# Loading pairs of row slabs as two 64-partition halves in a column-mean kernel

## Chip, cores and metric

The kernel runs on 1 core of one Trainium2 chip. The metric is device time in microseconds (us) of one launch. Three runs of the kernel before took 628.69, 629.22 and 629.66 us; the median is 629.22 us.

## The reference

```python
def setup_inputs():
    return {"x": np.random.randn(8192, 8192).astype(np.float32)}

def reference(x):
    return np.mean(x, axis=0)
```

The input is 8192 rows of 8192 floats, 268.4 MB, and each byte is read once. The output is one row of 8192 column means.

## The kernel before

The 8192 rows are seen as 64 slabs of 128 rows. Slabs are taken in pairs: 31 pairs (`n_pairs`, k = 0 to 30), and the last two slabs are handled by a separate tail.

A pair lives in one tile `pair` of 128 partitions by 16,384 floats (64 KB in each partition). Partition p holds two neighbouring rows of x, 2p and 2p + 1 of the pair's 256 rows, one after the other, so what one partition takes is 64 KB in one piece in memory. The pool `pair_pool` has 3 buffers, and the tail's tile is taken from the same pool.

The loop over k (lines 92 to 103) does three things for each pair. First, SyncE issues the pair's load (line 98). Most pairs are one load of 8 MB over all 128 partitions. Pair 0 is cut at column 2048 (`FIRST`), and the last three pairs (`BY_ROW`, k = 28 to 30) are cut at column 8192, into the first and the second row of each partition. Second, VectorE adds the first half of the previous pair to the first half of this pair. Third, except for the last pair, VectorE adds the second half of this pair onto its first half. Both adds work on 128 x 8192 floats (helper `add`, line 87). After the loop the running sum is in the first half of the last pair.

The load of pair k goes into the buffer that pair k - 3 had. That buffer is free when the first add of pair k - 2 has read it. The instructions stand in program order on each engine (`manual_schedule`), and all loads stand on SyncE's queue, q1.

The tail (lines 106 to 118) loads the second last slab in column pieces, among them one of 120 rows and one of 8 rows for columns 7680 to 8192 (`ROWS`, `SPLIT`, line 113), and the last slab in seven pieces of falling width (`PIECES`, line 116). TensorE multiplies the running sum and the tail's slabs by ones (line 65) to sum over partitions in PSUM; ScalarE and VectorE scale by 1/8192 (lines 80 and 82), and three small stores write the output.

Of the kernel before, what the change touches and what calls it, by code (L numbers as in the profile page):

```python
# [1 line left out]

# [4 lines left out]

F32 = mybir.dt.float32
ADD = mybir.AluOpType.add
GROUPS = 4  # L10

WIDE = (2048, 2048, 2048, 1024)
NARROW = (256, 256, 256, 256)
PIECES = (4096, 2048, 1024, 512, 256, 160, 96)
FIRST = 2048
BY_ROW = 3

ROWS = 120  # L20
SPLIT = 7680


@with_exitstack
def kernel(
    ctx: ExitStack,
    tc: tile.TileContext,
    x: bass.AP,
    out: bass.AP,
):  # L30
    nc = tc.nc
    P = nc.NUM_PARTITIONS
    R, C = x.shape
    n_slabs = R // P
    n_pairs = n_slabs // 2 - 1
    N0 = sum(WIDE)
    assert n_slabs % 2 == 0 and n_pairs >= 4 and N0 + sum(NARROW) == sum(PIECES) == C
    inv_r = 1.0 / float(R)

    const_pool = ctx.enter_context(tc.tile_pool(name="const", bufs=1))  # L40
    pair_pool = ctx.enter_context(tc.tile_pool(name="pair", bufs=3))
    psum_pool = ctx.enter_context(
        tc.tile_pool(name="acc", bufs=1, space=bass.MemoryType.PSUM)
    )
    res_pool = ctx.enter_context(tc.tile_pool(name="res", bufs=1))


    ctx.enter_context(tc.manual_schedule())

    ones = const_pool.tile([P, 32], F32)  # L50
    nc.gpsimd.memset(ones, 1.0)  # L51

    wide, lo = [], 0
    for n, w in enumerate(WIDE):
        bank = psum_pool.tile([P, w // GROUPS], F32, name=f"wide{n}", tag=f"wide{n}")
        wide.append((lo, w, bank))
        lo += w
    narrow = []
    for n, w in enumerate(NARROW):
        bank = psum_pool.tile([P, 512], F32, name=f"narrow{n}", tag=f"narrow{n}")  # L60
        narrow.append((lo, w, 32 * n, bank))
        lo += w

    def mm(dst, src, **flags):
        nc.tensor.matmul(out=dst, lhsT=ones, rhs=src, skip_group_check=True, **flags)  # L65

    def fold_wide(n, src, **flags):
        lo, w, bank = wide[n]
        q = w // GROUPS
        for g in range(GROUPS):  # L70
            a = lo + g * q
            mm(bank[32 * g : 32 * g + 32, :], src[:, a : a + q], **flags)

    def fold_narrow(n, src, lo, hi, **flags):
        at, _, g, bank = narrow[n]
        mm(bank[g : g + 32, lo - at : hi - at], src[:, lo:hi], **flags)

    def scaled(dst, src, eng):
        if eng == "act":
            nc.scalar.mul(out=dst, in_=src, mul=inv_r)  # L80
        else:
            nc.vector.tensor_scalar(  # L82
                out=dst, in0=src, scalar1=inv_r, scalar2=None, op0=mybir.AluOpType.mult
            )

    def add(dst, a, b):
        nc.vector.tensor_tensor(out=dst, in0=a, in1=b, op=ADD)  # L87

    before = None
    for k in range(n_pairs):
        pair = pair_pool.tile([P, 2 * C], F32, tag="pair")
        src = x[2 * P * k : 2 * P * (k + 1), :].rearrange("(p j) c -> p (j c)", j=2)
        cut = FIRST if k == 0 else C if k >= n_pairs - BY_ROW else 2 * C
        for lo, hi in ((0, cut), (cut, 2 * C)):
            if lo < hi:
                nc.sync.dma_start(out=pair[:, lo:hi], in_=src[:, lo:hi])  # L98
        if before is not None:
            add(pair[:, 0:C], pair[:, 0:C], before[:, 0:C])  # L100
        if k < n_pairs - 1:
            add(pair[:, 0:C], pair[:, 0:C], pair[:, C : 2 * C])
        before = pair


    tail = pair_pool.tile([P, 2 * C], F32, tag="pair")
    r = (n_slabs - 2) * P
    slab, last = tail[:, 0:C], tail[:, C : 2 * C]
    parts = [(lo, lo + w) for lo, w, _ in wide[:3]] + [(wide[3][0], C)]
    for lo, hi in ((0, C // 2), (C // 2, SPLIT)):  # L110
        nc.sync.dma_start(out=slab[:, lo:hi], in_=x[r : r + P, lo:hi])
    for a, b in ((0, ROWS), (ROWS, P)):
        nc.sync.dma_start(out=slab[a:b, SPLIT:C], in_=x[r + a : r + b, SPLIT:C])
    lo = 0
    for w in PIECES:
        nc.sync.dma_start(out=last[:, lo : lo + w], in_=x[r + P : R, lo : lo + w])
        lo += w


    for lo, hi in parts:  # L120
        add(before[:, lo:hi], before[:, lo:hi], before[:, C + lo : C + hi])
    lo, hi = parts[3]
    add(before[:, lo:hi], before[:, lo:hi], slab[:, lo:hi])

    rw = res_pool.tile([P, 3 * 512], F32, name="rw")
    r3 = res_pool.tile([P, WIDE[3] // GROUPS], F32, name="r3")
    row = res_pool.tile([1, C - N0], F32, name="row")

    def close(n):
        fold_wide(n, last, start=False, stop=True)  # L130
        scaled(rw[:, n * 512 : (n + 1) * 512] if n < 3 else r3, wide[n][2], "act")

    for n in range(3):
        fold_wide(n, before, start=True, stop=False)
        fold_wide(n, slab, start=False, stop=False)
    fold_wide(3, before, start=True, stop=False)
    for n, (lo, w, _, _) in enumerate(narrow):
        fold_narrow(n, before, lo, lo + w, start=True, stop=False)
    for n in range(4):
        close(n)  # L140
    W3 = 3 * GROUPS * 512
    nc.gpsimd.dma_start(  # L142
        out=out[0:W3].rearrange("(n g w) -> g n w", g=GROUPS, w=512),
        in_=rw.rearrange("(g r) (n w) -> g r n w", r=32, w=512)[:, 0],
    )
    nc.sync.dma_start(
        out=out[W3:N0].rearrange("(g w) -> g w", g=GROUPS),
        in_=r3.rearrange("(g r) w -> g r w", r=32)[:, 0],
    )
    for n, (lo, w, g, bank) in enumerate(narrow):  # L150
        if n < 3:
            fold_narrow(n, last, lo, lo + w, start=False, stop=True)
        else:
            cut = C - PIECES[-1]
            fold_narrow(n, last, lo, cut, start=False, stop=True)
            fold_narrow(n, last, cut, C, start=False, stop=True)
        scaled(row[0:1, lo - N0 : lo - N0 + w], bank[g : g + 1, 0:w], "act" if n % 2 else "dve")
    nc.sync.dma_start(out=out[N0:C], in_=row)


# [1 line left out]
_INS = ['x']  # L162
_OUTS = [((8192,), 'float32')]


# [23 lines left out]
```

## Time and profile before

| what | value |
|---|---|
| timed runs (median; lowest to highest) | 629.22 us; 628.69 to 629.66 us |
| span of the profiled execution, first to last instruction | 627.3 us |
| time around the span, taken as median less span | 1.9 us |
| DMA engines | near fully busy throughout; 428 GB/s over the span |
| VectorE busy | 533.5 us, 85% of the span |
| TensorE busy | 13.0 us, 2% |
| pair loads (line 98) | 35, of which 27 are of 8 MB |
| granted TensorE clock | 0.999 |

The profile states a span for the profiled execution and no separate device time, so its own time is taken as 627.3 us plus the 1.9 us that the median of the timed runs stands above it.

In the profile's page, section 2 cuts the span into 40 equal slices and gives the bytes moved per second in each; section 3 gives the DMA queues; section 4 follows the chain of work that ended last; section 5 lists groups of instructions with what ended the idle time before them; section 6 lists the DMA issues. The trace also holds a record of every DMA packet with its start, length and bytes; a packet here is one run of bytes that one of the 16 DMA engines moves.

### The profile page before, as it was taken

How to read it: one execution, taken by the hardware profiler on the slowest of the kernel's cores; microseconds unless marked ns; L12 is line 12 of the kernel's file. 1: busy time of each engine (PE TensorE's matmuls, PEld its weight loads, DVE VectorE, ACT ScalarE, POOL GpSimd, SP SyncE). 2: the span in 40 equal slices, each digit the busy share in tenths (PEclk: the TensorE clock that was granted, in tenths of full speed). 3: DMA queues.
4: the chain of work that ended last, by engine and by line, in shares of the span. 5: the costliest groups of instructions: out<-in, count | busy, mean ns of one | idle time of the engine just before them, and what ended most of it. 6: DMA issues, size and time to landing. Idle time of an engine off the chain costs nothing.

```text
span 627.3 us, 451 instructions
## 1 busy us (share of the span) xinstructions
PE 13.0 (2%) x106; PEld 3.8 (1%) x106; DVE 533.5 (85%) x67; ACT 4.2 (1%) x7; POOL 1.0 (0%) x6
## 2 busy tenths in 40 slices
PE   0000000000000000000000000000000000000016
PEld 0000000000000000000000000000000000000001
DVE  0538988889888899888898888988889888899994
ACT  0000000000000000000000000000000000000001
POOL 0000000000000000000000000000000000000000
PEclk9999999999999999999999999999999999999999
DMA  9999999999999999999999999999999999999997
GB/s 414 396 460 401 468 401 468 401 451 418 443 426 430 439 426 443 418 451 410 460 405 464 401 468 401 468 402 468 401 468 401 468 401 468 401 433 435 435 421 287
DMA packets 6548, 268.50 MB, mean 428 GB/s; under 512 B 900, under 2 KB 1160, under 8 KB 1553
## 3 DMA queue, kind: packets, MB, share of 16 engines
q1 hardware_dynamic: 6497, 268.45, 99.2%
q0 software_dynamic: 48, 0.02, 0.0%
q8 instruction: 1, 0.02, 0.0%
q14 instruction: 2, 0.02, 0.0%
HBM read 268.44 MB, written 0.03 MB: 428 GB/s over the span
## 4 chain that ended last, share of the span: by engine, by line
DMA 77%; DVE 22%; PE 0%; issue 0%; SPq 0%; ACT 0%; DVEq 0%
DMA pair<-in_x_dram 72%; DVE pair L87 22%; DMA tail<-in_x_dram 5%; PE narrow L65 0%; SPq L98 0%; PE wide L65 0%; ACT row L80 0%; DVEq L87 0%
## 5 line engine op out<-in xcount | busy, mean ns | idle before, releaser
L87 DVE TENSOR_TENSOR pair<-pair 128x8192 f32<-128x8192 f32 (+1 forms) x64 | 530.4, 8292 | 85.2 <-DMA pair<-in_x_dram 84.1
L65 PE MATMUL wide<-pair,ones 128*32 128x512 f32 (+1 forms) x32 | 4.8, 679 | 610.8 <-DVE pair L87 610.8
L65 PE MATMUL wide<-tail,ones 128*32 128x512 f32 (+1 forms) x56 | 7.7, 634 | 0.7 <-DMA tail<-in_x_dram 0.7
L82 DVE TENSOR_SCALAR row<-narrow 1x256 f32<-1x256 f32 x2 | 0.8, 416 | 6.2 <-PE narrow L65 6.1
L80 ACT ACTIVATE rw<-wide 128x512 f32<-128x512 f32 x3 | 1.8, 597 | 619.5 <-PE wide L65 619.5
L65 PEld LDWEIGHTS wide<-pair,ones 128*32 128x32 f32 x32 | 1.1, 134 | 613.5 <-issue 610.3
L87 DVE TENSOR_TENSOR pair<-pair,tail 128x2048 f32<-128x2048 f32 x1 | 2.3, 2292 | 0.0
L65 PEld LDWEIGHTS wide<-tail,ones 128*32 128x32 f32 x56 | 1.7, 119 | 6.1 <-issue 3.1
L142 POOL DMA_DIRECT2D out_dram<-rw x1 | 0.7, 695 | 622.7 <-ACT rw L80 622.7
L80 ACT ACT_TABLE_LOAD x1 | 1.3, 1283 | 0.7 <-PEq L173 0.7
L65 PE MATMUL narrow<-tail,ones 128*32 128x256 f32 (+2 forms) x10 | 1.2, 346 | 0.0
L80 ACT ACTIVATE row<-narrow 1x256 f32<-1x256 f32 x2 | 0.8, 376 | 0.4 <-PE narrow L65 0.2
L65 PEld LDWEIGHTS narrow<-tail,ones 128*32 128x32 f32 x10 | 0.6, 108 | 0.8 <-DMA tail<-in_x_dram 0.6
L65 PE MATMUL narrow<-pair,ones 128*32 128x256 f32 x8 | 0.6, 379 | 0.0
L80 ACT ACTIVATE r<-wide 128x256 f32<-128x256 f32 x1 | 0.4, 384 | 0.2 <-PE wide L65 0.2
L65 PEld LDWEIGHTS narrow<-pair,ones 128*32 128x32 f32 x8 | 0.3, 110 | 0.2
L51 POOL MEMSET ones<- 128x32 f32 x1 | 0.1, 124 | 0.3 <-POOLq L173 0.3
L173 POOL MEMSET const-float32-0.0<- 128x1 f32 x1 | 0.1, 98 | 0.2 <-issue 0.2
L173 POOL MEMSET const-float32-1.0<- 128x1 f32 x1 | 0.1, 98 | 0.0
L173 POOL MEMSET const-bfloat16-1.0<- 128x1 bf16 x1 | 0.1, 98 | 0.0
L173 POOL MEMSET const-uint8-127<- 128x1 uint8 x1 | 0.1, 98 | 0.0
## 6 DMA issues: line engine op xcount, KB each, us to landing
pair<-in_x_dram SPq DMA_DIRECT2D x6, 4096.0 KB, 25.8
pair<-in_x_dram SPq DMA_DIRECT2D x1, 7168.0 KB, 21.1
tail<-in_x_dram SPq DMA_DIRECT2D x2, 2048.0 KB, 19.2
tail<-in_x_dram SPq DMA_DIRECT2D x1, 1792.0 KB, 24.0
pair<-in_x_dram SPq DMA_DIRECT2D x1, 1024.0 KB, 4.7
tail<-in_x_dram SPq DMA_DIRECT2D x1, 1024.0 KB, 30.2
tail<-in_x_dram SPq DMA_DIRECT2D x1, 512.0 KB, 28.8
pair<-in_x_dram SPq DMA_DIRECT2D x27, 29.8
```

The costliest lines, as they stand in the source:

```text
L51: nc.gpsimd.memset(ones, 1.0)
L65: nc.tensor.matmul(out=dst, lhsT=ones, rhs=src, skip_group_check=True, **flags)
L80: nc.scalar.mul(out=dst, in_=src, mul=inv_r)
L82: nc.vector.tensor_scalar(out=dst, in0=src, scalar1=inv_r, scalar2=None, op0=mybir.AluOpType.mult)
L87: nc.vector.tensor_tensor(out=dst, in0=a, in1=b, op=ADD)
L142: nc.gpsimd.dma_start(out=out[0:W3].rearrange("(n g w) -> g n w", g=GROUPS, w=512), in_=rw.rearrange("(g r) (n w) -> g r n w", r=32, w=512 ...
L173: nc = _bacc.Bacc("TRN2", target_bir_lowering=False, num_devices=1)
```

## The change

Pairs 0 to 27 are loaded in two loads, of partitions 0 to 63 and of partitions 64 to 127, in place of one over 128 partitions. Pair 0, which was already cut at column 2048, becomes four loads. Pairs 28 to 30 are still two loads of 128 partitions each, but the first now takes the pair's first 128 rows and the second its last 128 rows, instead of the first and second of two neighbouring rows. What is added to what, the sizes of the tiles, the adds and the tail stay as they are.

```diff
     for k in range(n_pairs):
         pair = pair_pool.tile([P, 2 * C], F32, tag="pair")
-        src = x[2 * P * k : 2 * P * (k + 1), :].rearrange("(p j) c -> p (j c)", j=2)
-        cut = FIRST if k == 0 else C if k >= n_pairs - BY_ROW else 2 * C
-        for lo, hi in ((0, cut), (cut, 2 * C)):
-            if lo < hi:
-                nc.sync.dma_start(out=pair[:, lo:hi], in_=src[:, lo:hi])
+        r = 2 * P * k
+        if k >= n_pairs - BY_ROW:
+            for j in range(2):
+                nc.sync.dma_start(
+                    out=pair[:, j * C : j * C + C], in_=x[r + j * P : r + j * P + P, :]
+                )
+        else:
+            src = x[r : r + 2 * P, :].rearrange("(p j) c -> p (j c)", j=2)
+            for lo, hi in ((0, FIRST), (FIRST, 2 * C)) if k == 0 else ((0, 2 * C),):
+                for a in (0, P // 2):
+                    b = a + P // 2
+                    nc.sync.dma_start(out=pair[a:b, lo:hi], in_=src[a:b, lo:hi])
         if before is not None:
             add(pair[:, 0:C], pair[:, 0:C], before[:, 0:C])
```

## The prediction

> **What bounds the kernel now.** I read the page first: the busy shares and slices, then the chain that ended last, then the groups, then the chain in order of time, SyncE's waits, and the packet records behind the slices.
>
> ```profile
> PE 13.0 (2%) x106; PEld 3.8 (1%) x106; DVE 533.5 (85%) x67; ACT 4.2 (1%) x7; POOL 1.0 (0%) x6
> DMA  9999999999999999999999999999999999999997
> DMA packets 6548, 268.50 MB, mean 428 GB/s; under 512 B 900, under 2 KB 1160, under 8 KB 1553
> q1 hardware_dynamic: 6497, 268.45, 99.2%
> DMA 77%; DVE 22%; PE 0%; issue 0%; SPq 0%; ACT 0%; DVEq 0%
> L87 DVE TENSOR_TENSOR pair<-pair 128x8192 f32<-128x8192 f32 (+1 forms) x64 | 530.4, 8292 | 85.2 <-DMA pair<-in_x_dram 84.1
> ```
>
> The 16 DMA engines are busy in every slice but the last. VectorE is busy 85% and idles 84.1 us, always for a pair's landing. The 22% of VectorE on the chain are not a second bound: the chain passes through an add because it frees a buffer. In order of time one turn of it is
>
> ```profile
> 119.84 8.70 DVE pair L87
> 128.54 0.02 issue
> 128.56 29.99 DMA pair<-in_x_dram
> 158.54 0.03 issue
> ...
> 545.65 8.70 DVE pair L87
> ```
>
> The load issued at 128.56 lands 29.99 us later, though 8.39 MB need 19.3 us at the engines' rate: it first waits about 10 us behind the load before it. So the queue never runs dry, and one pair lands every 19.3 us (from 158.64 to 197.24 are two turns, 38.60). In steady stages, by the windows,
>
> ```profile
> 200.00:400.00 200.00, 0.00 (x0) 0.00 (x0) 180.57 (x22) 0.00 (x0) 0.00 (x0) 1.00 1.00 435
> 25.00:60.00 35.00, 0.00 (x0) 0.00 (x0) 23.52 (x3) 0.00 (x0) 0.00 (x0) 1.00 0.97 419
> ```
>
> the last column is 435 GB/s in the long stage and 419 in the early one. By the packet records nearly every 64 KB packet takes 2.418 us, 3,092 of 3,456 to the nanosecond, which is 27.1 GB/s per engine and 434 for 16. The bound is the rate at which the engines write into the tiles.
>
> **The landmarks for the sum.** The first packet starts at about 1.8 us; pair 27 lands at 545.6 (the add at 545.65 waits for it); 81.7 us are left to the end of the span. So 28 pairs take 543.8 us, 19.42 each. The time is the span, 627.3, plus 1.9 us around it up to the median.
>
> **More loads on SyncE.** Pairs 0 to 27 go from 29 loads to 58 (pair 0 from two to four), the last three keep two each: 35 issues become 64.
>
> ```profile
> L98 SPq DMA_DIRECT2D pair<-in_x_dram x35: 327/328/576, 0.7 to 572.2; - x35
> SPq L98 <- DVE pair L87: 537.5, 28, 28.2
> ```
>
> An issue costs 0.33 us, at the start 0.4. The 29 more are some 12 us, but SyncE waits 537.5 us for VectorE, and a pair's second issue stands behind no other wait; the load ahead in the queue has 10 us to go, so 0.4 us is hidden. Were that cover gone, it would cost 28 x 0.4 = 11 us. At the start the two 512 KB loads of pair 0 need 2.4 us at 435 GB/s against 0.8 us to issue the next two: nothing. The add now waits for two landings; SyncE's own semaphore instruction takes 17 ns, so 28 x 0.02 = 0.6 us on VectorE, which idles 2 us ahead of each pair: nothing. VectorE's adds do not change.
>
> **The last three pairs.** Six loads of 4 MB in 32 KB packets become six loads of 4 MB in 32 KB packets; only the pitch of the rows read is halved, to 32 KB. The tail already reads 16 KB packets at that pitch, at 611 ns, which is full rate (26.8 GB/s). Cost nothing, gain nothing. From the landing of pair 27 on, the order of loads, adds and buffers is the same, so the 81.7 us move as a block.
>
> **The halves themselves.** This is the whole question: does a load over 64 partitions still run at 16 x 27.1 GB/s? No row of before shows 64 partitions. The nearest is the tail's load of 120 rows by 2 KB (line 113), the only big load that is not over 128. In the packet records it is spread as 8 rows on each of 15 engines, and the 8-row load behind it as one row on each of 8; so a 64-row load should be 4 rows on each of 16 engines. All loads of 128 rows around it, of 1 to 16 KB a row, run at their nominal length, and at the switch from one to the next nothing is stretched. After the 120-row load 14 of its 15 engines (the other runs late) take 976 to 1,079 ns for their first 16 KB packet (nominal 611), about 715 for the second and about 635 for the third; with the last 2 KB packets, 84 ns grown to 95 to 134, that is some 590 ns too much for each engine. Each of them had moved 16 KB of that load, nominally 0.64 us. So the load cost 1.92 times its time, the excess showing late, as if writes had piled up. The windows show the dip:
>
> ```profile
> 604.00:608.00 4.00, 0.00 (x0) 0.00 (x0) 3.97 (x2) 0.00 (x0) 0.00 (x0) 1.00 1.02 436
> 612.00:615.00 3.00, 3.00 (x28) 0.89 (x24) 3.00 (x2) 0.00 (x0) 0.00 (x0) 1.00 1.08 371
> ```
>
> [...]
>
> Bounds for one pair: below, nothing, or a gain of 0.14 us if halves kept 435 GB/s throughout (8.39 MB / 435 = 19.28 against 19.42; 28 x 0.14 = 4 us); above, all 16 engines halved, 2 x 19.3 = 38.6 us. By the 120-row load itself, 1.92 x 19.3 = 37.1. I take the halving: in that load one of fifteen engines may be alone and its neighbours lie apart in time, whereas a 64-row load gives 16 engines half of the partitions for many microseconds. [...] Leads in this trace are up to 0.5 us, but the pair of engines with the smallest lead sets the landing: I take 0.1 us, for 56 halves 5 us.
>
> Sum: 1.8 + 28 x 38.6 + 81.7 = 1,164, less 5 = 1,159 us span; plus 1.9: **1,161 us**. With 37.1 per pair and no leads it would be 1,124. The DVE no longer matters: 17.4 us of adds against 38.6 of load. Own range of this case 1,110 to 1,185; the top is 2 x 19.42 for each pair, 1,173, and 1% for the changes between halves.
>
> **Rival 1: no slower, because an engine is the limit and not the partitions.** Then all 16 engines run 2.418 us packets whatever they write to, halves simply follow each other in the queue, and the sum is unchanged: 629 us, at best 625 with the 4 us above. For it: the 27.1 GB/s is seen per engine everywhere, and no 64-row load is there to contradict. Against it: the stretched packets. It decides if the 64 KB packets stay at 2.42 us. [...] Chance 0.11.
>
> [...] Chance 0.10, spread from 670 to 1,110.
>
> **Rival 3: the load uses only eight engines**, eight rows on each as in the 128-row loads. Then 8 x 27.1 = 217 GB/s, again 38.6 us a pair, without leads: 1,166 us. It is inside the main case, and would show as 2.42 us packets on half of the engines.
>
> **How the numbers follow.** Main case with rival 3: 0.76. Rival 2: 0.10. Rival 1: 0.11. Something else slower, such as a loss at each change of half or below two thirds of the doubling: 0.03. The range 950 to 1,190 holds the main case, the slow end of rival 2 and some of the rest: about 0.81; all of rival 1 is left out. A measurement of this kernel can tell 0.2% (1.3 us) from no change. Of rival 1, 0.03 is faster by that much, 0.07 the same, and 0.01 slower; with the other cases slower is 0.90.
>
> **What would show it.** Right: 64 KB packets at about 4.8 us; slices near 217 GB/s up to the last three of 40 and near 435 after that; VectorE's busy time still 533 us but idle for over 600 us, for pair landings; the chain almost all DMA; the first add of pair 1 at about 79 us instead of 41.9, and 38.6 us between turns; 81.7 us from pair 27 to the end. The step on the last three pairs is wrong if their packets leave 1.21 us; the step on SyncE, if DMA engines go idle before a second half. The prediction is wrong outright if slices stay above 400 GB/s, and its size is wrong if the time between landings shrinks along the run.

## The result, and the profile after

The changed kernel takes 1,222.63 us (median of 5 runs, 1,221.47 to 1,223.95) against 629.22 us before. The ratio is 1.9436, with a 95% interval of 1.9415 to 1.9457. The prediction had the halved rate and the direction, but 1,222.6 lies above its range, which ended at 1,190.

From the page after: the busy shares, the DMA slices, the packets, the queue, the chain and the largest group.

```profile
span 1221.4 us, 482 instructions
PE 12.7 (1%) x106; PEld 3.8 (0%) x106; DVE 533.5 (44%) x67; ACT 4.2 (0%) x7; POOL 1.0 (0%) x6
DMA  9999999999999999999999999999999999999898
GB/s 215 197 206 206 206 206 206 206 206 206 206 206 206 206 206 206 212 204 223 200 217 206 210 206 208 206 208 206 204 206 208 206 206 206 206 206 206 343 434 358
DMA packets 7012, 268.51 MB, mean 220 GB/s; under 512 B 1364, under 2 KB 1624, under 8 KB 2017
q1 hardware_dynamic: 6961, 268.45, 99.7%
another core or an unknown queue 52%; DVE 40%; DMA 7%; issue 0%; PE 0%; SPq 0%; DVEq 0%; ACT 0%
L87 DVE TENSOR_TENSOR pair<-pair 128x8192 f32<-128x8192 f32 (+1 forms) x64 | 530.4, 8291 | 679.6 <-DMA pair<-in_x_dram 678.5
```

The engines are as busy as before and move half as much: 206 GB/s until the last three slices, then up to 434, where loads of 128 partitions begin. VectorE works the same 530.4 us on the pairs and now waits 678.5 us for landings. The 52% of "another core or an unknown queue" are those landings: the add now waits for two loads, and the chain no longer finds one releaser. The idle row names the load.

One turn of the chain in order of time, and SyncE's side:

```profile
84.21 8.70 DVE pair L87
92.91 0.02 issue
92.94 8.69 DVE pair L87
101.63 23.07 another core or an unknown queue
124.70 0.03 issue
...
1139.93 0.03 issue
L105 SPq DMA_DIRECT2D pair<-in_x_dram x58: 465/594/599, 0.7 to 1068.2; - x58
SPq L105 <- DVE pair L87: 995.0, 25, 49.4
```

A pair lands every 40.61 us (84.21 to the next first add, 23.07 us of waiting behind 17.4 us of adds). Pair 27 lands at 1,139.9, and 81.5 us are left. An issue of a 64-partition load takes 0.594 us, more than the 0.33 of a 128-partition load, hidden by 995 us of waiting. By the packet records all 3,456 packets of 64 KB take 4.89 to 5.43 us, 5.08 in the mean. Three in four take 5.13; the fourth, on most engines the first of each half, takes 4.94. Before it was 2.418.

### The profile page after: what moved, and what is told of

It reads as the page before. It is cut to its first block, busy times and chain, and to the rows that moved or that the text cites. A ratio compares the mean times of both kernels' runs of the same rounds, so it can differ in the third digit from the quotient of the medians.

```text
span 1221.4 us, 482 instructions
## 1 busy us (share of the span) xinstructions
PE 12.7 (1%) x106; PEld 3.8 (0%) x106; DVE 533.5 (44%) x67; ACT 4.2 (0%) x7; POOL 1.0 (0%) x6
## 4 chain that ended last, share of the span: by engine, by line
another core or an unknown queue 52%; DVE 40%; DMA 7%; issue 0%; PE 0%; SPq 0%; DVEq 0%; ACT 0%
DVE pair L87 40%; DMA pair<-in_x_dram 5%; DMA tail<-in_x_dram 2%; SPq L105 0%; DVEq L87 0%; PE narrow L65 0%; PE wide L65 0%; ACT row L80 0%
## 5 line engine op out<-in xcount | busy, mean ns | idle before, releaser
L87 DVE TENSOR_TENSOR pair<-pair 128x8192 f32<-128x8192 f32 (+1 forms) x64 | 530.4, 8291 | 679.6 <-DMA pair<-in_x_dram 678.5
```

## The experiments

The expectations call W the author's theory that the partitions a load writes set how long its packets take, and not the size or the number of the loads. All runs go from the first load to the stores; e5, e6 and e12 leave some rows out. Where no interval is given there is one timed run.

**e1: twice the loads, all 128 partitions.** On the kernel before:

```diff
-        cut = FIRST if k == 0 else C if k >= n_pairs - BY_ROW else 2 * C
+        cut = FIRST if k == 0 else C
```

> Every pair is loaded in two loads of 128 partitions and 32 KB per row, cut by column, so that the number of loads, the bytes of a load (4 MB) and the second wait are those of the changed kernel, but not its partitions. [...] Rival N (a load of half the bytes, or one more load per pair, costs about 10 us each time): about 1,222 us.

630.39 us, ratio to before 1.0022 (1.0013 to 1.0032). From its page:

```profile
GB/s 417 394 428 430 434 434 434 434 434 434 434 434 434 434 434 432 434 434 430 434 432 432 432 432 434 434 434 434 432 434 430 426 432 434 434 432 434 434 426 278
```

The number of loads, their 4 MB and the second wait cost 1.2 us in all, where at most 1 was expected. Rival N is out. Where the 1.2 us go was not followed up.

**e2, e3, e4: other cuts of the 128 partitions.** On the changed kernel, the line `for a in (0, P // 2)` was replaced, one form for each run:

```diff
-                for a in (0, P // 2):
-                    b = a + P // 2
+                for a, b in ((0, P // 4), (P // 4, 3 * P // 4), (3 * P // 4, P)):    # e2
+                for a in range(0, P, P // 4):    # e3, b = a + P // 4
+                for a in range(0, P, P // 8):    # e4, b = a + P // 8
```

> Pairs 0 to 27 in three loads: partitions 0 to 31, 32 to 95, 96 to 127. The middle load has 64 partitions, half below and half above 64. [...] Rival R (any load of 64 rows or fewer runs at half rate, since an engine has few rows of it): all packets 5.1 us, about 1,222 us. Rival N (per load): two more loads a pair, 28 x 62 + 85 = 1,820 us.

> Pairs 0 to 27 in four loads of 32 partitions. An engine has two rows of each load. [...] Rival N (per load): 28 x 83 + 85 = 2,410 us.

> Pairs 0 to 27 in eight loads of 16 partitions. An engine has one row of each load. [...] Rival R (few rows per load, half rate): about 1,222 us. Rival N (per load): 28 x 168 + 85 = 4,790 us.

e3 takes 1,222.12 us with 64 KB packets of 5.08 us in the mean: four loads of 32 partitions are as fast as two of 64. e4 takes 2,182.91 us with packets of 9.36, both under what was expected (2,252 to 2,387 us, 9.7 to 10.3). The windows of e3 and then e4 (last column GB/s):

```profile
200.00:400.00 200.00, 0.00 (x0) 0.00 (x0) 86.92 (x10) 0.00 (x0) 0.00 (x0) 1.00 0.99 204
```

```profile
200.00:400.00 200.00, 0.00 (x0) 0.00 (x0) 52.15 (x6) 0.00 (x0) 0.00 (x0) 1.00 0.99 110
```

Rival N, which wanted 2,410 and 4,790 us, and rival R, which wanted 1,222 for both, fall. The 64 KB packets take 2.418 us in loads of 128 partitions, 5.082 in the mean at 64 and 5.08 at 32, and 9.363 at 16. Loads of 64 partitions thus lose 5% against the plain doubling of 2.418 us in the mean, and 6% in the packets of 5.13 us; loads of 32 lose 5% as well; loads of 16 lose nothing against four times 2.418 us. Why e4 has no loss isn't shown: its loads also change partitions more often, and in the changed kernel the packet behind a change of half takes 4.94 us and not 5.13.

e2 is a miss: 1,139.36 us where 931 was expected. Its 64 KB packets run from 2.418 us, as forecast for the middle load, to 8.4, with a mean of 4.15, and its engines idle:

```profile
q1 hardware_dynamic: 7425, 268.45, 88.9%
```

Some packets do reach the full rate (2.418 us) from a 64-partition load. In the records from 300 to 380 us most engines move together and then stand idle, while two or three others are out of step with packets of up to 7.5 us; the next load seems to wait for these. So the middle load was tried by itself.

**e5, e6, e12: one 64-partition load a pair, placed in two ways.** Half of the rows of pairs 3 to 26 is not loaded. On the changed kernel:

```diff
+        part = 3 <= k <= 26
...
-                for a in (0, P // 2):
-                    b = a + P // 2
+                for a, b in ((32, 96),) if part else ((0, P),):    # e5; e6: ((0, 64),)
...
-            add(pair[:, 0:C], pair[:, 0:C], before[:, 0:C])
-        if k < n_pairs - 1:
+            q = slice(32, 64) if 3 <= k <= 27 else slice(0, P)     # e6: slice(0, 32)
+            add(pair[q, 0:C], pair[q, 0:C], before[q, 0:C])
+        if k < n_pairs - 1 and not part:
```

> Pairs 3 to 26 load only partitions 32 to 95, in one load of 64 partitions; the other half of their rows is left out, and so are their adds but one of 32 partitions. Pairs 0 to 2 and 27 to 30 are loaded over 128 partitions. [...] Rival R (a load of 64 rows runs at half rate wherever it lies): 20.3 us a pair, 650 us, the same as the run with partitions 0 to 63.

> The same kernel, with partitions 0 to 63 in place of 32 to 95; half of the rows of pairs 3 to 26 is left out in the same way. Theories W and R: packets of 5.13 us, 20.3 us a pair, 1.8 + 4 x 19.4 + 24 x 20.3 + 82 + 2 = 651 us. If the 6% above the doubling came from the change between lower and upper half, which is not there now, packets of 4.84 us and 627 us.

e5 431.13 us, e6 656.11. The windows of e5, then of e6:

```profile
100.00:300.00 200.00, 0.00 (x0) 0.00 (x0) 162.43 (x19) 0.00 (x0) 0.00 (x0) 1.00 0.94 388
```

```profile
100.00:300.00 200.00, 0.00 (x0) 0.00 (x0) 86.79 (x10) 0.00 (x0) 0.00 (x0) 1.00 1.01 206
```

The same bytes, rows per engine and number of loads: 2.42 us a packet in e5 (the first of each load mostly 2.7 to 3.3, behind a queue that runs dry while the load waits for an add; 396 to 415 us was expected with packets of 2.42 us, and I put the 16 us above 415 down to this) and 5.13 in e6 (the first of each load 5.08). So 64 partitions go at the full rate at 32 to 95, half below and half above 64, and not at 0 to 63. e6 never changes halves and still has 5.13, so the 6% is not from the change between halves; in the changed kernel the packet behind a change is even shorter (4.94 against the 5.08 of the first of each load here).

e5 also read other rows than e6. e12 is e5 with its partitions filled from the rows that e6 read:

```diff
-                    nc.sync.dma_start(out=pair[a:b, lo:hi], in_=src[a:b, lo:hi])
+                    o = 32 if part else 0
+                    nc.sync.dma_start(out=pair[a:b, lo:hi], in_=src[a - o : b - o, lo:hi])
```

> As the run with partitions 32 to 95 alone (e5), but these partitions are filled from rows 0 to 127 of each pair, the rows that e6 read into partitions 0 to 63; half of the rows of pairs 3 to 26 is left out. If the partitions written decide: 64 KB packets of 2.42 us, 431 us as e5. If the addresses read decide: packets of 5.13 us, 656 us as e6.

442.43 us, 64 KB packets of 2.42 in the median. Its window, against 388 GB/s in e5 and 206 in e6:

```profile
100.00:300.00 200.00, 0.00 (x0) 0.00 (x0) 155.66 (x18) 0.00 (x0) 0.00 (x0) 1.00 0.91 372
```

The partitions written decide, not the addresses read: these rows took 5.13 us a packet in e6. The 11 us over e5 come with more idle DMA time; why was not followed up.

**e7, e11: does a lead between engines help?** An extra load at the head of the changed kernel, whose data are not used, one row of 64 KB on each of eight engines in e7 and of three in e11:

```diff
+    ahead = pair_pool.tile([P, 2 * C], F32, tag="pair")
+    nc.sync.dma_start(
+        out=ahead[0:8, :], in_=x[0:16, :].rearrange("(p j) c -> p (j c)", j=2)    # e11: ahead[0:3], x[0:6]
+    )
```

Theory D: the engines with a row of it start behind the others, this lead lasts, and packets of engines in different halves get shorter, to 2.42 us in e7 (635 to 670 us) and to between 2.4 and 4.9 on some engines in e11. That a lead shortens packets was the author's estimate.

> [...] Rival S (the engines fall back into step, since the next load is only given when the slowest has landed): packets back at 5.1 us after some pairs, about 1,200 to 1,230 us.

> [...] In all cases the other engines set the landings: 1,222 to 1,232 us.

e7 1,234.18 us, e11 1,231.53: the expected gain did not come in either. In e7 the late engines stay late: eight of them begin each half 3.6 us behind the other eight at the start and still at 980 us. So the two groups are in different halves for 3.6 of every 20.3 us, yet no 64 KB packet is under 4.92 us. In e11 three engines still write their last 56 KB packet of the upper half when the 13 others have moved to the lower one; they take 4.43 to 4.45 us for it, against 4.49 in the median of the changed kernel and 2.116 in a load of 128. Theory D falls, and S does not describe it either: the lead stays and buys nothing. The head of e7 has engines slowed beside a load in which they have no row: while the extra load runs, the eight engines without a row of it take 1.21 to 1.25 us for 8 KB packets, where the changed kernel's first loads have 0.59 in the median.

**e13: the extra load ahead of loads of 128 partitions.** The extra load of e7 at the head of the kernel before, where the loads around it are of 128 partitions. Two outcomes were set against each other: while the extra load runs, the engines without a row of it take 1.0 to 1.3 us for an 8 KB packet, held up like the others (theory J), or they stay at 0.31. About 637 us was expected with the first and 635 to 639 with the second.

> The kernel before with the extra load of e7 at its head: 8 rows of 64 KB into partitions 0 to 7, one on each of eight engines; its data are not used. [...]

638.38 us. In the packet records the eight engines without a row of the extra load take 1.21 to 1.25 us for 8 KB packets from 4.7 us of the span on, all eight of them, after about 1 us in which the packets grow; about 1 us after the extra load has ended, at 10.7 us, they are back at 0.309 us. The windows around the extra load show what all other packets moved meanwhile, and the rate afterwards:

```profile
5.00:11.00 6.00, 0.00 (x0) 0.00 (x0) 0.00 (x0) 0.00 (x0) 0.00 (x0) 1.00 0.60 67
20.00:40.00 20.00, 0.00 (x0) 0.00 (x0) 8.60 (x1) 0.00 (x0) 0.00 (x0) 1.00 1.01 440
```

(A packet counts where it starts; those of the extra load started earlier.) 67 GB/s is far below 8 x 27.1 = 217, an estimate of what eight engines move at the 2.418 us of before. So theory J holds for this case, an extra load to partitions 0 to 7: the engines without a row of it go about as slowly as those with one (64 KB in 7.7 to 9.0 us). It may be the reason in e11 too, where three engines stay slow while 13 write the other half; that was not shown.

It is no general rule, as the records of e2 show. There, for 54 us in all, at least twelve engines are in packets of 2.42 us while at least two others are in packets of over 4.5 us. So slow engines don't always hold up the rest. What makes the difference was not tried: to how few partitions the slow engines write, or how many engines they are. For e7 the reason is open too, and what held the engines up was not found.

**e8: the halves on two queues.** On the changed kernel:

```diff
-                    nc.sync.dma_start(out=pair[a:b, lo:hi], in_=src[a:b, lo:hi])
+                    (nc.scalar if a else nc.sync).dma_start(out=pair[a:b, lo:hi], in_=src[a:b, lo:hi])
```

> The changed kernel with the loads of partitions 64 to 127 issued by ScalarE's queue, those of 0 to 63 by SyncE's. An engine then takes packets from both queues in turn. [...]

1,184.15 us, 64 KB packets of 4.91 in the mean:

```profile
q1 hardware_dynamic: 4641, 151.01, 53.2%
q10 hardware_dynamic: 2320, 117.44, 46.5%
200.00:400.00 200.00, 0.00 (x0) 0.00 (x0) 90.78 (x11) 0.00 (x0) 0.00 (x0) 1.00 1.01 215
```

1,222 us with packets of 5.1 was expected if all engines go from half to half in step, and 630 to 700 with packets of 2.42 if they do not. The packets are those of the first case, but with 1.5% above the doubling in place of 5%. The second queue itself need not be the reason. In the records the engines take one packet from q1 and one from q10 in turn, so nearly every packet follows one to the other half. In the changed kernel the packet behind a change of half takes 4.94 us, and in e3 4.93, close to the 4.91 here. So most of the loss sits in packets that follow another to the same half. Why is open.

**e9: the other part of the change alone,** pairs 28 to 30 as slabs of 128 rows, with `for a, b in ((0, P),)` in place of the halves.

> The kernel before with the second part of the change alone: pairs 28 to 30 loaded as slabs of 128 rows, all other pairs in one load of 128 partitions. Every theory: 32 KB packets of 1.213 us in the last three pairs as before, no difference, 629 us within 0.6.

628.93 us, ratio 0.9999 (0.9990 to 1.0008). No difference is seen, as the prediction had it.

**e10: the row that the forecast was built on.** On the kernel before, the tail's load of 120 rows and that of 8 joined into one:

```diff
-    for lo, hi in ((0, C // 2), (C // 2, SPLIT)):
+    for lo, hi in ((0, C // 2), (C // 2, SPLIT), (SPLIT, C)):
         nc.sync.dma_start(out=slab[:, lo:hi], in_=x[r : r + P, lo:hi])
-    for a, b in ((0, ROWS), (ROWS, P)):
-        nc.sync.dma_start(out=slab[a:b, SPLIT:C], in_=x[r + a : r + b, SPLIT:C])
```

> The kernel before with the tail's 120-row and 8-row loads joined into one load of 128 rows by 2 KB. [...]

If the stretched 16 KB packets came from the load of 120 rows, none over 0.65 us and some 0.5 us less were expected; by rival P they came from the switch to the last slab or from the pitch of the rows read, and would stay. Of 257 packets of 16 KB, 37 took over 0.65 us before and one does here; the stretch, 9.1 us summed over the packets before (0.57 us an engine), is 0.3 us. So the stretched packets came from the load cut into 120 and 8 rows, and rival P is out. The time is 628.81 us, ratio 0.9996 (0.9987 to 1.0005): the 0.5 us is not told from nothing, and no faster version of the kernel comes of it.

## Why the prediction was right and where it was wrong

**The halves.** Right in that 64 partitions of one half are loaded at about half the rate: packets go from 2.418 us to 5.08 in the mean, and the bound moves from 435 GB/s to 206. That the rate depends on which partitions are written is shown by e5, e6 and e12 (packets of 2.42, 5.13 and 2.42 us), and e3 and e4 agree (5.08 and 9.36). What in the chip makes it so no run shows. That the stretch came from the 120-row load is borne out by e10.

**The term that was mis-sized** is "I take the halving", 2 x 19.3 = 38.6 us a pair, that is, a plain doubling without loss. There is a loss: a pair takes 40.61 us, 28 x 2.01 = 56 us in all. The prediction's other estimate, 37.1 us a pair, is further off. The 120-row load did not show the loss: its 1.92 was below 2. That a slowing of only half a microsecond was too short to show it is a guess. I took 2, plus 1%, as the end of the range where it was only the lossless value; no row of before bounded the time of a 64-partition load from above.

**The second term, the 5 us taken off for leads,** is shown by no run: that a lead of one engine over another is saved in each half was the author's estimate. What the runs show in its place is that the packet behind each change of half is 0.19 us shorter than the others, over 56 halves 11 us. The 56 us are net of this; at 5.13 us throughout, the loss would be 67. A lead did not save time: in e11 three engines that were alone in their half saved next to nothing (4.43 to 4.45 us against 4.49), and in e7 a lead of 3.6 us in each half, some 200 us over 56, saved none. So that the size came near is luck.

**The sum.** Landing of pair 27: 1,139.9 against 1,077.6 predicted. That is 67 from packets of 5.13 us in place of 2 x 2.418, 6 less because changes of half saved 11 and not 5, and 1 from the start, where an issue now takes 0.6 us. Afterwards 81.5 against 81.7, and around the span 1.2 against 1.9. That is the 61.6 us between 1,161 and 1,222.6 to within rounding. The range's top allowed 1% for "the changes between halves"; the changes saved time, and e6 has its 5.13 us without any.

**What held.** 29 more issues are hidden, though each costs 0.594 and not 0.33 us. The last three pairs cost nothing (e9). The second wait costs nothing (e1 has it, and 1.2 us in all). VectorE's busy time is unchanged, and the block from pair 27 to the end moved as one.

**The rivals.** Rival 1, the engine as the limit, is out by the packets of 5.1 us. Rival 2, that the engines drift out of step and packets then get shorter, did not happen: in e7 a lead of 3.6 us neither grew nor paid. A lead of a whole half was in no run. Rival 3, eight engines at 2.42 us, is out: no 64 KB packet was under 4.89. What set the size, packets 5% longer than the doubling, was not among them; it fell to the 0.03 of "something else slower".

**Open.** What makes the time depend on the partitions written; why packets that follow one to the same half take 6% more than the doubling and those behind a change of half only 1.5 to 2%; why e4 has no loss; what holds up the engines without a row of the extra load in e13 and three engines in e11, but not twelve in e2; why e7's lead paid nothing.

## What to carry to other kernels

Look at which partitions a load covers, not only at its bytes. Here 128 partitions went at 435 GB/s and halves at 206, so keep such loads on the full 128, and where it must be 64, try 32 to 95 (64 KB packets of 2.42 us) ahead of 0 to 63 (5.13). To bound a rate from a short load, look at the packets that follow it too, and do not take the lossless share as the worst case: leave room above it, here 5%. A load to few partitions can slow engines that have no row of it (8 KB in 1.21 to 1.25 us for 0.309 in e13): look at their packets too.

## What was not expected of the hardware

- A load of 64 partitions runs at the full rate at 32 to 95 (packets of 2.42 us) and at less than half of it at 0 to 63 (5.13 us); at 32 to 95 the packets took 2.42 us with the rows of either load.
- In loads of one half the packets take more than twice as long as in loads of 128 partitions (5.08 us in the mean against 2 x 2.418): 64 KB take 5.13 us behind a packet to the same half and 4.91 to 4.94 behind one to the other half.
- A load can slow engines that have no row of it: an extra load of 8 rows to partitions 0 to 7 took the eight engines without a row of it from 0.309 to between 1.21 and 1.25 us for an 8 KB packet. In e2 at least twelve engines ran at 2.42 us for 64 KB beside at least two at over 4.5, so it isn't always so.
- An issue of a 64-partition load takes 0.594 us on SyncE against 0.328 for one of 128 partitions.
